# Reading out a state-space scan one step later, and holding a table's transpositions for its rotation table

## The chip, the cores and the metric

One core of one Trainium2 chip runs the whole computation as one program. The metric is the device time of one execution in microseconds (us); three runs of the kernel before gave a median of 2172.66 us (2171.47 to 2174.1).

## The reference

Two layers of a block in which four token mixers work side by side on quarters of the width: latent attention (MLA), grouped-query attention (GQA), a state-space mixer (SSM) and a gated long convolution (hyena). There are 1024 latent and 256 context tokens of width 1024, all in fp32. Cut to what matters here:

```python
for l in range(2):
    h = rms_norm(x) * (1 + scale) + shift          # latent and context
    p = h @ w_in[l]                                # 2912 columns
    a = mla(p); g = gqa(p); s = ssm(p); y = hyena(p)
    x = x + gate * rms_norm(concat(a, g, s, y) @ w_out[l])

# ssm, 16 groups of 16 channels, 64 complex states each, two directions:
bu = einsum('bngh,gph->bngp', u, b_bar)            # drive
s_t = a_bar * s_(t-1) + bu_t                       # linear_scan, over context and then latent tokens
y = einsum('bngp,ghp->bngh', s, c).real            # readout, both directions added
out = gelu(y + d * u) * sigmoid(...) * silu(gate)  # finish
```

## The kernel before

The kernel is written with a tile framework that takes the program's instructions, simulates them with its own clock, and lays down one order for each engine. Each engine then works its list in order and waits at an instruction until the semaphores of what that needs have come. Priorities follow the order in which the code issues things; what is put under `high_priority` goes first, and the scheduler fills the rest of an engine's list with whatever its simulation holds to be ready. So a wait added at one place can shift instructions far from it.

In each layer the stages are: input projection `ipc` (three fp32r matmuls for each fp32 product, from high and low parts of activations and weights), run in blocks of columns of which the last eight, the gates, are written last and are filler for TensorE; hyena's filter (`hps`, `fdft`, `cdft`); the SSM's tables; the SSM's recurrence; hyena's convolution (`hytr`, `ldft`, `lout`; for the context in layer 0 `hcd`, `hco`, `hcz`); the preparation of queries, keys and values (`mqn`, `mkn`, `mv` and others); the SSM's finish (`sglu`); then attention (`aS`, `acx`, `apt`, `apo`), the output projection and the next layer's normalisation. Between the stages data pass through HBM, and all loads and stores (L201) are issued by SP, one list in order. The lanes stand in the order state space, preparation, finish, hyena in layer 0, and hyena, state space, preparation, finish in layer 1. A stage's pools reuse the memory of earlier ones and wait for them.

**Tables** (`ssm_tables`, four groups of four): for each group VectorE and GpSimd form E and Fm (`sE`, `sF`), three products and sums each for the real and the imaginary part. TensorE transposes E (`etp`, L253; eight transpositions for a group), ScalarE copies the result, E times C gives the short kernel (`kfp`). Then the rotation table `tab` (`sT`) is formed in the same way from two tables of powers. E, Fm and their transposed copy have one buffer each. `mtp` builds the direct term's matrices from all groups, and everything goes to HBM.

**Recurrence** (`ssm`, eight steps of two groups): `drive` loads the step's tables, multiplies U by E^T (`drv`) and copies the drive into D in scan order. `scan` turns D by the rotation table (products `cm` on GpSimd, the others on VectorE), runs the two scans (`sV`), and turns the states back into D (`sD`). `read` adds, in one PSUM tile `sy`, the direct term `smt` x U and the states' part `sfm` x D, six matmuls for a step, and ScalarE copies it over U. Step k+1's drive is issued before step k's scan; D has two buffers, Fm (`sfm`) two, the direct term `mt` (`smt`) one. The loop of the kernel before:

```python
d = drive(0)
for gc in range(N):
    e = drive(gc + 1) if gc + 1 < N else None
    yield
    scan(gc, *d)
    yield
    read(gc, d[1], *R)
```

Of the kernel before, what the change touches and what calls it, by code (L numbers as in the profile page):

```python
# [11 lines left out]
F32 = mybir.dt.float32  # L12
# [8 lines left out]
ADD, SUB, MUL = ALU.add, ALU.subtract, ALU.mult  # L21
# [166 lines left out]
class K:  # L188
# [32 lines left out]
        return self.psf.tile([128, 512], F32, tag="f", name=name)  # L221

    def mm(self, out, lhsT, rhs, start=True, stop=True):
        self.keep(self.nc.tensor.matmul(out, lhsT, rhs, start=start, stop=stop))  # L224

    def mm3(self, out, a, b, start, stop):

# [2 lines left out]
        self.mm(out, a[1], b[0], False, stop)  # L230

    def tt(self, out, a, b, op, eng=None):
        self.keep((eng or self.nc.vector).tensor_tensor(out=out, in0=a, in1=b, op=op))  # L233

    def stt(self, out, a, s, b, op0, op1):
        self.keep(self.nc.vector.scalar_tensor_tensor(out=out, in0=a, scalar=s, in1=b, op0=op0, op1=op1))  # L236
# [13 lines left out]

    def tr(self, out, in_):
        p = in_.shape[0]
        self.keep(self.nc.tensor.transpose(out, in_, self.ident[:p, :p]))  # L253


    def setup(self, es):
# [869 lines left out]
    def ssm_tables(self, l, P, poles):  # L1126
# [20 lines left out]
        for gc in range(4):  # L1147
            gs = slice(gc * G, gc * G + G)
            E = P.tile([128, 2, G, 8, 16], F32, tag="sE", name="sE")
            Fm = P.tile([128, 2, G, 8, 16], F32, tag="sF", name="sF")  # L1150
            sh = [128, G, 8, 16]
            for dst, pk, vec, sg in ((E, pe, bb, 1.0), (Fm, pf, cw, -1.0)):
                kr, ki = (pk[:, i, :, gs].rearrange("p t g -> p g t").unsqueeze(3).to_broadcast(sh) for i in range(2))
                vr, vi = (vec[:, i, gs, :].unsqueeze(2).to_broadcast(sh) for i in range(2))
                w1 = P.tile(sh, F32, tag="sw0", name="sw1")
                w2 = P.tile(sh, F32, tag="sw1", name="sw2")
                tt(dst[:, 0], kr, vr, MUL)
                tt(w1, ki, vi, MUL)
                tt(dst[:, 0], dst[:, 0], w1, SUB)
                tt(dst[:, 1], kr, vi, MUL, pool)  # L1160
                tt(w2, ki, vr, MUL, pool)
                if sg > 0:
                    tt(dst[:, 1], dst[:, 1], w2, ADD, pool)
                else:
                    stt(dst[:, 1].rearrange("p g t h -> p (g t h)"), dst[:, 1].rearrange("p g t h -> p (g t h)"), -1.0,
                        w2.rearrange("p g t h -> p (g t h)"), MUL, SUB)

            yield
            et = P.tile([128, 2, G, 128], F32, tag="sET", name="sET")
            for ri in range(2):  # L1170
                ps = self.b1("etp")
                for g in range(G):
                    self.tr(ps[:, g * 128:g * 128 + 128], E[:, ri, g].rearrange("p t h -> p (t h)"))
                nc.scalar.copy(et[:, ri].rearrange("p g c -> p (g c)"), ps)
            self.store(eD[:, :, gs], et)
            self.store(fD[:, :, gs], Fm.rearrange("p r g t h -> p r g (t h)"))
            kp = self.b1("kfp").rearrange("p (g c) -> p g c", c=32)
            for g in range(G):
                for ri in range(2):
                    self.mm(kp[:, g, :], E[:, ri, g].rearrange("p t h -> p (t h)"), cp[:, ri, gc * G + g, :], ri == 0, ri == 1)  # L1180
            nc.vector.tensor_copy(kfb[:, :, gs, :].rearrange("p d g h -> p g d h"),
                                  kp[:, :G, :].rearrange("p g (d h) -> p g d h", d=2))

            tab = P.tile([128, 2, G, 16, 10], F32, tag="sT", name="sT")
            sh = [128, G, 16, 10]
            ar, ai = (big[:, i, gs].unsqueeze(3).to_broadcast(sh) for i in range(2))
            br, bi = (small[:, i, gs].unsqueeze(2).to_broadcast(sh) for i in range(2))
            w1 = P.tile(sh, F32, tag="sw0", name="sr0")
            w2 = P.tile(sh, F32, tag="sw1", name="sr1")
            tt(tab[:, 0], ar, br, MUL)  # L1190
            tt(w1, ai, bi, MUL)
            tt(tab[:, 0], tab[:, 0], w1, SUB)
            tt(tab[:, 1], ar, bi, MUL, pool)
            tt(w2, ai, br, MUL, pool)
            tt(tab[:, 1], tab[:, 1], w2, ADD, pool)
            self.store(tD[:, :, gs], tab.rearrange("p r g a b -> p r g (a b)"))
            yield

        pad = P.tile([128, 352], F32, tag="sw0", name="pad")
# [13 lines left out]
    def ssm(self, l, P, uD, yD, tabs, ctx):  # L1213
# [11 lines left out]
        def readout(gc):  # L1225
            gs = slice(gc * G, gc * G + G)
            Fm = P.tile([128, 2, G, 128], F32, tag="sfm", name="sfm", bufs=2)
            mt = P.tile([128, G, 128], F32, tag="smt", name="smt")
            self.load(Fm, fD[:, :, gs])
            self.load(mt, mD[:, gs])  # L1230
            return Fm, mt
# [11 lines left out]
        def drive(gc):  # L1243
            gs = slice(gc * G, gc * G + G)
            tb = P.tile([128, 2, G, 160], F32, tag="stb", name="stb", bufs=2)
            et = P.tile([128, 2, G, 128], F32, tag="set", name="set")
            self.load(et, eD[:, :, gs])
            self.load(tb, tD[:, :, gs])
            D = P.tile([128, 2, G, 160], F32, tag="sD", name="sD", bufs=2)
            for ri in range(2):  # L1250
                ps = self.b1("drv")[:, :G * 160].rearrange("p (g c) -> p g c", g=G)
                for g in range(G):
                    self.mm(ps[:, g, :], et[:, ri, g, :], U[:, gc * G + g, :])
                nc.scalar.copy(D[0:64, ri], ps[0:64])
                nc.scalar.copy(D[64:128, ri, :, 0:32], ps[64:128, :, 31::-1])
                nc.scalar.copy(D[64:128, ri, :, 32:160], ps[64:128, :, 159:31:-1])
            rt = P.tile([128, G, 160], F32, tag="sR", name="sR", bufs=2)
            for g in range(G):
                self.act(rt[:, g], ones, scale=rho[:, gc * G + g:gc * G + g + 1])
            return tb, D, rt  # L1260

        def scan(gc, tb, D, rt):
# [10 lines left out]
            c0, c1 = temp(0)[..., 0:159], temp(1)[..., 0:159]  # L1273
            tt(c0, V[:, 0], t1, MUL, nc.gpsimd)
            tt(c1, V[:, 1], t1, MUL, nc.gpsimd)
            tt(V[:, 0], V[:, 0], t0, MUL)
            tt(V[:, 1], V[:, 1], t0, MUL)
            f, b = slice(0, 64), slice(64, 128)
            if ctx:
# [6 lines left out]
                if ctx:  # L1286
                    tt(D[b, ri, :, 30::-1], V[b, ri, :, 0:31], c[b, :, 0:31], op)

        def read(gc, V, Fm, mt):
            gs = slice(gc * G, gc * G + G)  # L1290
            n = hi - lo
            ps = self.b1("sy")[:, :G * n].rearrange("p (g c) -> p g c", g=G)
            for g in range(G):
                self.mm(ps[:, g, :], mt[:, g, :], U[:, gc * G + g, lo:hi], True, False)
                self.mm(ps[:, g, :], Fm[:, 0, g, :], V[:, 0, g, lo:hi], False, False)
                self.mm(ps[:, g, :], Fm[:, 1, g, :], V[:, 1, g, lo:hi], False, True)
            nc.scalar.copy(U[:, gs, lo:hi], ps)
# [9 lines left out]

        N = 16 // G
        d = drive(0)
        for gc in range(N):  # L1310
            e = drive(gc + 1) if gc + 1 < N else None
            yield
            scan(gc, *d)
            yield
            read(gc, d[1], *R)
            yield
            if e:
                d, R = e, readout(gc + 1)

    def ssm_finish(self, l, P, uD, yD, ctx):  # L1320
        nc, A = self.nc, self.A
# [689 lines left out]
```

## Time and profile before

| | |
|---|---|
| median of three runs | 2172.66 us |
| the profiled execution's own time | 2168.31 us |
| its span, first to last instruction | 2166.5 us |
| TensorE (PE) busy | 1933.1 us, 89% |
| VectorE (DVE) busy | 1557.0 us, 72% |
| GpSimd (POOL) busy | 972.2 us, 45% |
| ScalarE (ACT) busy | 896.6 us, 41% |

The shares are means over stages with different limits. Layer 0's projections, tables, recurrence and preparation lie in about 75 to 737 us, its attention from 736.8, its output projection from about 1060; in layer 1 the same stretches start at about 1215, 1778 and 2066. The trace holds two records for an fp32 matmul and one for an fp32r matmul, so the counts of `lout`, `hco`, `sglu`, `drv`, `sy` and `etp` in it are twice those of the program; `ipc`, `mkn` and `aS` are counted once.

### The profile page before, as it was taken

To read this page: it belongs to the slowest core of one execution; us is meant where nothing else is said; L and a number is where in the kernel's file an instruction comes from. 1 tells how busy PE (TensorE), PEld (TensorE's weight loads), DVE (VectorE), ACT (ScalarE), POOL (GpSimd) and SP (SyncE) were. 2 spreads that over 40 slices of the span, in tenths; PEclk is the share of its full clock that TensorE was granted. 3 is DMA by queue.
4 is the path that set the end of the run, shared out by engine and by line. 5 is a ranking of instruction groups with operands and counts; after the bars stand their busy time and mean duration, and the time that the engine had idled before them with its cause. 6 is when DMAs were issued, how large, how long until landed. Compare 5 with 4: busy or idle time off the path is not lost.

```text
span 2166.5 us, 31419 instructions
## 1 busy us (share of the span) xinstructions
PE 1933.1 (89%) x10811; PEld 1602.2 (74%) x10811; DVE 1557.0 (72%) x2969; ACT 896.6 (41%) x1926; POOL 972.2 (45%) x782
## 2 busy tenths in 40 slices
PE   6988998899889599899998898988889979999888
PEld 2677887777768477788777677887766667899766
DVE  5699349757776488788653498479769868999721
ACT  2422234224234367667423222344224227788611
POOL 0757236584461144434156558246566624340034
PEclk9798899899999899999899998999899989999999
DMA  7323365337656545452343423364457675561063
GB/s 254 97 91 136 108 222 142 98 118 239 201 174 197 147 126 154 139 160 80 90 142 123 139 99 130 113 232 137 128 161 223 204 213 142 150 169 46 12 184 126
DMA packets 261280, 316.55 MB, mean 146 GB/s; under 512 B 46671, under 2 KB 203599, under 8 KB 257793
## 3 DMA queue, kind: packets, MB, share of 16 engines
q1 hardware_dynamic: 261120, 314.55, 47.6%
q8 instruction: 85, 1.39, 0.3%
q14 instruction: 75, 0.61, 0.1%
HBM read 207.61 MB, written 106.86 MB: 145 GB/s over the span
## 4 chain that ended last, share of the span: by engine, by line
PE 47%; DVE 29%; DMA 10%; issue 7%; POOL 3%; ACT 2%; SPq 2%; POOLq 0%; DVEq 0%; ACTq 0%
PE ipc L224 9%; PE apo L224 7%; PE apt L253 6%; PE aS L224 6%; PE ops L224 6%; DVE lU L233 3%; DVE sD L233 3%; PE mps L224 2%; SPq L201 2%; DVE sp L233 2%; PE acx L224 2%; PE fdft L224 2%; PE hps L224 1%; DVE lX L233 1%; DVE sV L233 1%
## 5 line engine op out<-in xcount | busy, mean ns | idle before, releaser
L224 PE MATMUL ipc<-hh,whi 128*128 128x512 f32 (+2 forms) x992 | 386.7, 390 | 31.4 <-DVE ipt L236 12.8
L224 PE MATMUL ipc<-hh,wlo 128*128 128x512 f32 (+2 forms) x992 | 381.5, 385 | 3.9 <-POOL wlo L233 3.9
L224 PE MATMUL ipc<-hl,whi 128*128 128x512 f32 (+2 forms) x992 | 382.9, 386 | 0.4 <-POOL hl L233 0.4
L224 PEld LDWEIGHTS ipc<-hh,whi 128*128 128x128 f32 x992 | 196.3, 198 | 65.8 <-DVE ipt L236 15.2
L233 DVE TENSOR_TENSOR aPl<-apt,aPh 128x512 fp32r<-128x512 f32 x328 | 223.8, 683 | 20.7 <-ACT aPh L1672 16.9
L1672 ACT CAST aPh<-apt 128x512 fp32r<-128x512 f32 x328 | 186.5, 590 | 124.2 <-PE apt L253 118.3
L224 PEld LDWEIGHTS ipc<-hh,wlo 128*128 128x128 f32 x992 | 196.5, 198 | 35.2 <-POOL wlo L233 4.6
L224 PEld LDWEIGHTS ipc<-hl,whi 128*128 128x128 f32 x992 | 196.9, 198 | 31.2 <-issue 3.8
L233 POOL TENSOR_TENSOR wlo<-wraw,whi 128x512 fp32r<-128x512 f32 x92 | 139.1, 1516 | 137.1 <-ACT whi L462 103.3
L253 PE MATMUL apt<-ident,aP 128*128 128x128 f32 x1312 | 190.5, 276 | 1.2 <-DVE aPl L233 1.0
L224 PE MATMUL aS<-kst,aq 128*128 128x512 f32 x512 | 152.3, 420 | 26.4 <-DMA aq<-gP 20.8
L1637 DVE TENSOR_REDUCE am<-aS 128x1 f32<-128x1024 f32 x128 | 155.5, 1215 | 21.7 <-PE aS L224 21.6
L246 ACT ACTIVATE aP<-aS,am,rs 128x1024 f32<-128x1024 f32 x128 | 155.5, 1215 | 33.5 <-DVE am L243 32.4
L1700 POOL COPY aLB<-am 128x128 f32<-128x128 f32 x72 | 21.0, 292 | 322.8 <-DVE am L1692 322.8
L253 PEld LDWEIGHTS apt<-ident,aP 128*128 128x128 f32 x1312 | 148.3, 141 | 16.7 <-DVE aPl L233 6.4
L224 PE MATMUL apo<-aPh,vst 128*128 128x256 f32 x656 | 138.3, 308 | 15.3 <-ACT aPh L1672 8.7
L224 PE MATMUL apo<-aPl,vst 128*128 128x256 f32 x656 | 123.5, 286 | 1.6 <-DVE aPl L233 1.3
L224 PEld LDWEIGHTS aS<-kst,aq 128*128 128x128 f32 x512 | 88.2, 192 | 41.7 <-issue 21.2
L224 PEld LDWEIGHTS apo<-aPh,vst 128*128 128x128 f32 x656 | 96.2, 190 | 30.6 <-DVE aob L233 15.8
L224 PE MATMUL ops<-owh,omh 128*128 128x512 f32 x288 | 93.5, 405 | 17.1 <-ACT omh L1785 10.8
L224 PEld LDWEIGHTS apo<-aPl,vst 128*128 128x128 f32 x656 | 100.3, 189 | 8.6 <-DVE aPl L233 3.8
L224 PE MATMUL ops<-owl,omh 128*128 128x512 f32 x288 | 93.3, 404 | 0.0
(369 smaller groups left out, 4382.4 us busy)
## 6 DMA issues: line engine op xcount, KB each, us to landing
wraw<-in_w_col_dram SPq DMA_DIRECT2D x64, 256.0 KB
mraw<-in_w_mod_dram SPq DMA_DIRECT2D x32, 512.0 KB
kst<-mK SPq DMA_DIRECT2D x16, 640.0 KB
omx<-mixD SPq DMA_DIRECT2D x18, 512.0 KB
ogt<-gD SPq DMA_DIRECT2D x18, 512.0 KB
k<-kt SPq DMA_DIRECT2D x16, 512.0 KB
lk<-k SPq DMA_DIRECT2D x8, 1024.0 KB
gD<-ipt SPq DMA_DIRECT2D x32, 256.0 KB
```

Of the source, the lines that this page charges most:

```text
L201: return self.nc.sync.dma_start(out=out, in_=in_)
L224: self.keep(self.nc.tensor.matmul(out, lhsT, rhs, start=start, stop=stop))
L233: self.keep((eng or self.nc.vector).tensor_tensor(out=out, in0=a, in1=b, op=op))
L246: self.keep(self.nc.scalar.activation(out=out, in_=in_, func=func, **k))
L253: self.keep(self.nc.tensor.transpose(out, in_, self.ident[:p, :p]))
L1637: self.keep(nc.vector.tensor_reduce(out=x["m"][:, 2 + qi:3 + qi], in_=x["S"][qi], axis=AX.X, op=ALU.max))
L1672: self.keep(nc.scalar.copy(h, ps))
L1700: self.keep(nc.gpsimd.tensor_copy(x["LB"][:, :, o:o + 64], x["m"][:, 10:12].unsqueeze(2).to_broadcast([128, 2, 64])))
```

## The change

The read-out of a step is held back: `scan` becomes a generator that stops after it has issued its product V times t0 (`sV`), and the read-out of the step before is issued there. Its first matmul gets a wait for that product (`behind`, a new dependency between two instructions that share no data). The last read-out follows the loop without a wait. D gets a third buffer and `mt` a second. In the tables the rotation table and its store move ahead of the transpositions, and the group's first transposition waits for the last subtraction of the table's real part. `mm`, `tt` and `tr` return their instruction.

```diff
+    def behind(self, ins, other):
+        self.tc.add_manual_dep(ins.ins, other.ins.name, mybir.DependencyInfo(
+            mybir.DependencyClass.Sync, mybir.DependencyReason.DATA), reason="behind")
...
             yield
+            tab = P.tile([128, 2, G, 16, 10], F32, tag="sT", name="sT")
...
+            last = tt(tab[:, 0], tab[:, 0], w1, SUB)
+            tt(tab[:, 1], ar, bi, MUL, pool)
+            tt(w2, ai, br, MUL, pool)
+            tt(tab[:, 1], tab[:, 1], w2, ADD, pool)
+            self.store(tD[:, :, gs], tab.rearrange("p r g a b -> p r g (a b)"))
             et = P.tile([128, 2, G, 128], F32, tag="sET", name="sET")
             for ri in range(2):
                 ps = self.b1("etp")
                 for g in range(G):
-                    self.tr(ps[:, g * 128:g * 128 + 128], E[:, ri, g].rearrange("p t h -> p (t h)"))
+                    ins = self.tr(ps[:, g * 128:g * 128 + 128], E[:, ri, g].rearrange("p t h -> p (t h)"))
+                    if ri == g == 0:
+                        self.behind(ins, last)
...
-            mt = P.tile([128, G, 128], F32, tag="smt", name="smt")
+            mt = P.tile([128, G, 128], F32, tag="smt", name="smt", bufs=2)
...
-            D = P.tile([128, 2, G, 160], F32, tag="sD", name="sD", bufs=2)
+            D = P.tile([128, 2, G, 160], F32, tag="sD", name="sD", bufs=3)
...
-            tt(V[:, 0], V[:, 0], t0, MUL)
+            yield tt(V[:, 0], V[:, 0], t0, MUL)
...
-        def read(gc, V, Fm, mt):
+        def read(gc, V, Fm, mt, other):
...
-                self.mm(ps[:, g, :], mt[:, g, :], U[:, gc * G + g, lo:hi], True, False)
+                ins = self.mm(ps[:, g, :], mt[:, g, :], U[:, gc * G + g, lo:hi], True, False)
+                if g == 0 and other is not None:
+                    self.behind(ins, other)
...
+        due = None
         for gc in range(N):
             e = drive(gc + 1) if gc + 1 < N else None
             yield
-            scan(gc, *d)
+            half = scan(gc, *d)
+            other = next(half)
+            if due:
+                read(*due, other)
             yield
-            read(gc, d[1], *R)
+            for _ in half:
+                pass
             yield
+            due = gc, d[1], *R
             if e:
                 d, R = e, readout(gc + 1)
+        read(*due, None)
+        yield
```

Three places of the laid-down order follow, first as it was, then as it is. TensorE in layer 0, at the third read-out `sy` of the recurrence; `drv` are drives, `hytr` and `ldft` hyena, `ipc` projections:

```order
L224 MATMUL drv<-sU,set 128x160 x2
L253 MATMUL hytr<-ident,hyx 128x128 x7
L224 MATMUL sy<-sU,smt 128x160
L224 MATMUL sy<-sD,sfm 128x160
L253 MATMUL hytr<-ident,hyx 128x128
L224 MATMUL sy<-sD,sfm 128x160
L224 MATMUL sy<-sU,smt 128x160
L224 MATMUL sy<-sD,sfm 128x160 x2
L224 MATMUL ipc<-bsel,sq 128x2 x7
```

The same place in the changed kernel:

```order
L224 MATMUL ldft<-hyt,hff 128x128 x4
L224 MATMUL sy<-sU,smt 128x160
L224 MATMUL sy<-sD,sfm 128x160 x2
L224 MATMUL sy<-sU,smt 128x160
L224 MATMUL sy<-sD,sfm 128x160 x2
L224 MATMUL drv<-sU,set 128x160 x2
L224 MATMUL ldft<-hyt,hff 128x128 x8
```

The third read-out stood among hyena's transpositions behind the drive of the fourth step; now it stands as one piece behind the drive of the fifth, the first half of the sixth step's drive following it.

SP in layer 0, from the last projections to attention; `hcz` is hyena's context product, `kst`, `vst` and `aq` are attention's keys, values and queries, `gD` a gate's store, `owr` and `mraw` are weights of later stages:

```order
L201 DMA owr<-in_w_out_dram 128x512 x2
L201 DMA gD_78<-ipt 128x256
L201 DMA owr<-in_w_out_dram 128x512 x2
L201 DMA mraw<-in_w_mod_dram 128x1024 x2
L201 DMA mixD_77<-hcz_5082 128x256
L201 DMA mraw<-in_w_mod_dram 128x1024
L201 DMA gpre<-in_g_pre_dram 128x8
L201 DMA bmt<-in_b_modT_dram 128x16
L201 DMA mixD_77<-hcz_5090 128x256
L201 DMA kst<-gP_4000 64x2560 x2
L201 DMA vst<-gV_4001 128x10x192
L201 DMA aq<-gP_4000 64x2x256 x6
```

The same place in the changed kernel:

```order
L201 DMA mixD_77<-sth 128x256 x2
L201 DMA gD_78<-ipt 128x512
L201 DMA mixD_77<-hcz_5082 128x256
L201 DMA mixD_77<-hcz_5090 128x256
L201 DMA gD_78<-ipt 128x512
L201 DMA kst<-gP_4000 64x2560 x2
L201 DMA vst<-gV_4001 128x10x192
L201 DMA gD_78<-ipt 128x256
L201 DMA aq<-gP_4000 64x2x256 x6
L201 DMA owr<-in_w_out_dram 128x512 x4
L201 DMA mraw<-in_w_mod_dram 128x1024 x3
```

Both stores of `hcz` now stand together, and `owr` and `mraw` behind the first queries. On TensorE of layer 0 the last eight `hco`, which feed `hcz`, had nothing between them and attention; now 28 `ipc` stand there.

TensorE in layer 1, where attention begins; `sglu` is the finish of the state-space mixer:

```order
L224 MATMUL ipc<-hh,whi 128x512
L224 MATMUL ipc<-hl,whi 128x512
L224 MATMUL ipc<-hh,wlo 128x512
L224 MATMUL sglu<-sz,sgw 128x256 x4
L224 MATMUL aS<-kst,aq 128x512 x4
L224 MATMUL sglu<-sz,sgw 128x256 x4
L224 MATMUL acx<-kst,aq 128x256 x4
```

The same place in the changed kernel:

```order
L224 MATMUL ipc<-hh,whi 128x512
L224 MATMUL ipc<-hl,whi 128x512
L224 MATMUL ipc<-hh,wlo 128x512
L224 MATMUL sglu<-sz,sgw 128x256 x4
L224 MATMUL aS<-kst,aq 128x512 x4
L224 MATMUL sglu<-sz,sgw 128x256 x12
L224 MATMUL acx<-kst,aq 128x256 x4
```

Of the sixteen `sglu` of this layer, the earlier ones had `ipc` between them; now all sixteen stand behind the last `ipc`. Between the last `mkn` of the preparation and the last `ipc` stood 99 `ipc` and 16 `lout`; now 43 `ipc` stand there.

## Rows read from the trace of the kernel before

**Rows 1.** Page, part 1: busy us (share of the span) xinstructions, by engine

```profile
PE 1933.1 (89%) x10811; PEld 1602.2 (74%) x10811; DVE 1557.0 (72%) x2969; ACT 896.6 (41%) x1926; POOL 972.2 (45%) x782
```

**Rows 2.** Stretches: length; PE, PEld, DVE, ACT, POOL busy (instructions); PEclk, DMA share, GB/s

```profile
250.00:300.00 50.00, 47.55 (x279) 40.23 (x278) 5.56 (x18) 14.05 (x36) 7.20 (x9) 1.00 0.42 129
350.00:400.00 50.00, 38.54 (x199) 34.18 (x197) 49.11 (x56) 13.38 (x36) 34.56 (x31) 0.90 0.42 115
1450.00:1500.00 50.00, 43.09 (x274) 39.26 (x273) 48.81 (x69) 26.34 (x62) 31.93 (x27) 0.96 0.71 234
1550.00:1750.00 200.00, 175.12 (x833) 134.74 (x832) 163.16 (x216) 62.93 (x142) 136.81 (x95) 0.96 0.63 194
1750.00:1790.00 40.00, 29.82 (x123) 23.30 (x121) 20.91 (x53) 11.40 (x27) 0.20 (x1) 0.83 0.84 229
```

**Rows 3.** Who TensorE waited for: us in total, times, longest us

```profile
PE sy L224 <- DVE sD L233: 17.5, 12, 5.4
...
PE sy L224 <- POOL wlo L233: 5.9, 2, 4.2
...
PE etp L253 <- DVE sE L233: 4.4, 2, 3.7
...
PE sy L224 <- POOL dd L233: 2.6, 1, 2.6
...
PE etp L253 <- ACT hsq L246: 2.4, 1, 2.4
```

**Rows 4.** Tile sD, 290 to 430: ns min/median/max, first and last start, forms

```profile
L224 PE MATMUL sy<-sD,sfm x64: 299/299/632, 309.9 to 417.3; 128*128 128x160 f32 x64
L233 DVE TENSOR_TENSOR sD<-sV,cm x48: 215/475/2357, 307.4 to 415.9; 64x318 f32<-64x318 f32 x16, 64x256 f32<-64x256 f32 x16, 64x62 f32<-64x62 f32 x16
...
L233 DVE TENSOR_TENSOR sD<-sD,stb x16: 475/492/1552, 298.1 to 407.1; 128x320 f32<-128x320 f32 x16
```

**Rows 5.** Tile sU, 270 to 300: its loads on SP

```profile
L201 SPq DMA_DIRECT2D sU<-uD x32: 303/429/1337, 274.8 to 291.1; - x32
```

**Rows 6.** Chain of waits, end of layer 0: start us, us, what

```profile
708.24 3.34 PE ipc L224 x26
...
713.10 1.58 PE hco L224 x6
...
715.15 7.03 DMA mixD<-hcz
...
722.75 0.33 SPq L201
...
726.86 9.78 DMA aq<-gP
...
736.77 2.05 PE aS L224 x4
```

**Rows 7.** DMA between 711 and 740 us: sum, and two kinds of load

```profile
DMA packets 4428, 7.30 MB, mean 252 GB/s; under 512 B 624, under 2 KB 3056, under 8 KB 4298
...
kst<-gP SPq DMA_DIRECT2D x2, 640.0 KB
...
vst<-gV SPq DMA_DIRECT2D x1, 960.0 KB
```

**Rows 8.** Chain of waits, whole span: a load by itself

```profile
972.67 2.35 DMA aq<-mS
```

**Rows 9.** Tile mkn, 1600 to 1760: TensorE's instructions

```profile
L224 PE MATMUL mkn<-sp,ukvh x16: 278/283/287, 1636.3 to 1736.7; 128*128 128x256 f32 x16
```

**Rows 10.** Tile sgy, 1740 to 1790: its loads on SP

```profile
L201 SPq DMA_DIRECT2D sgy<-yD x8: 319/395/545, 1746.3 to 1778.9; - x8
```

**Rows 11.** Chain of waits, end of layer 1

```profile
1750.99 3.06 PE lout L224 x24
...
1756.93 5.13 PE ipc L224 x22
...
1784.70 3.80 PE sglu L224 x8
```

More of the change, by code (lines that the diff above doesn't have):

```diff
@@ L223, in mm @@
     def mm(self, out, lhsT, rhs, start=True, stop=True):
-        self.keep(self.nc.tensor.matmul(out, lhsT, rhs, start=start, stop=stop))
+        ins = self.nc.tensor.matmul(out, lhsT, rhs, start=start, stop=stop)
+        self.keep(ins)
+        return ins
     def mm3(self, out, a, b, start, stop):
@@ L232, in tt @@
     def tt(self, out, a, b, op, eng=None):
-        self.keep((eng or self.nc.vector).tensor_tensor(out=out, in0=a, in1=b, op=op))
+        ins = (eng or self.nc.vector).tensor_tensor(out=out, in0=a, in1=b, op=op)
+        self.keep(ins)
+        return ins
+    def behind(self, ins, other):
+        self.tc.add_manual_dep(ins.ins, other.ins.name, mybir.DependencyInfo(
+            mybir.DependencyClass.Sync, mybir.DependencyReason.DATA), reason="behind")
     def stt(self, out, a, s, b, op0, op1):
@@ L252, in tr @@
         p = in_.shape[0]
-        self.keep(self.nc.tensor.transpose(out, in_, self.ident[:p, :p]))
+        ins = self.nc.tensor.transpose(out, in_, self.ident[:p, :p])
+        self.keep(ins)
+        return ins
     def setup(self, es):
@@ L1168, in ssm_tables @@
             yield
+            tab = P.tile([128, 2, G, 16, 10], F32, tag="sT", name="sT")
+            sh = [128, G, 16, 10]
+            ar, ai = (big[:, i, gs].unsqueeze(3).to_broadcast(sh) for i in range(2))
+            br, bi = (small[:, i, gs].unsqueeze(2).to_broadcast(sh) for i in range(2))
+            w1 = P.tile(sh, F32, tag="sw0", name="sr0")
+            w2 = P.tile(sh, F32, tag="sw1", name="sr1")
+            tt(tab[:, 0], ar, br, MUL)
+            tt(w1, ai, bi, MUL)
+            last = tt(tab[:, 0], tab[:, 0], w1, SUB)
[3 more added lines that the diff above has]
+            self.store(tD[:, :, gs], tab.rearrange("p r g a b -> p r g (a b)"))
             et = P.tile([128, 2, G, 128], F32, tag="sET", name="sET")
@@ L1182, in ssm_tables @@
                                   kp[:, :G, :].rearrange("p g (d h) -> p g d h", d=2))
[L1184 to L1196, printed above, removed]
             yield
```

## Prediction

> **What bounds the kernel now.** I read the busy shares first, then the stretches in which the change lies, then who waits for whom, then the chain of waits at the two places where a layer passes from its projections to attention. TensorE is busy for 89% of the span, VectorE for 72% [rows 1], so at first sight whatever takes a wait from TensorE is won. The stretches say otherwise. While the state-space recurrence runs beside the hyena convolution, VectorE has no idle time left: 49.11 of 50 us in layer 0, 48.81 of 50 in layer 1, with TensorE at 38.54 and 43.09 there [rows 2]. So TensorE's waits in this part are paid for VectorE's work, and they end when that work ends, wherever the waiting instruction stands. In 250 to 300 us it is the other way round: VectorE 5.56, TensorE 47.55 [rows 2]. TensorE's waits that the edit aims at are 17.5 + 5.9 + 2.6 = 26.0 us in front of `sy` (read-outs) and 4.4 + 2.4 = 6.8 us in front of `etp` (table transpositions) [rows 3]. 32.8 us is 1.5% of the span, and the most that the edits by themselves can give.
>
> **The change part by part.** The number of instructions is the same on every engine. What moves is their order, and the scheduler's answer to two new waits reaches far beyond the edited lines.
>
> *Read-outs.* In the row of TensorE, read-out k stood behind the drive of step k+1; it now stands behind that of step k+2, all six matmuls together. The states that it reads come from one step earlier, so that wait is gone, and the new one is for VectorE's V times t0 in the middle of the next scan. Behind a waiting `sy` stand the next drive, hyena transforms and projection matmuls, and for the drive wait ScalarE's copies and then GpSimd and VectorE of the scan after it. The matmuls of eight read-outs lie between 309.9 and 417.3 us, 15.3 us a step [rows 4]. But VectorE needs from its first scan instruction at 298.1 to the last at 415.9 [rows 4] whatever TensorE does, and the last two read-outs of each layer have no further step behind which to hide: in layer 0 they now stand next to each other. Ends: 0 (all of the wait comes back at the last read-outs) and -26.0. I take -4, near the zero end, as the row nearest to it is VectorE at 49.11 of 50.
>
> *Buffers and loads of the read-outs.* The third D and the second mt cost memory only. The mt and Fm loads for a read-out now wait in SP's queue for an older read-out; behind them stand the next step's table loads and weight loads. A load lands in 2.35 us when little is ahead of it [rows 8] and a step is 15.3 us: 0, with a step lost (15.3) only if the queue stands still until the read-out wants them.
>
> *Table transpositions.* The first `etp` of layer 0 stands 110 TensorE instructions later, the last one 88; in layer 1 the last stands 43 later. In place of `sE` they wait for the last subtraction of VectorE's rotation table, behind the six products of E and Fm, so by then E is long there. The stall of 6.8 goes, but each group's E buffer is now held until table, transposition and product are through, and the layer's table chain ends later. Ends: -6.8 and, if that chain delays the recurrence by as much, +6.8. I take -2: VectorE, which the recurrence needs, idles between the tables and the recurrence anyhow (5.56 of 50 busy in 250 to 300 [rows 2]).
>
> *What the scheduler puts in the gap.* With the tables later, the hyena loads stand ahead of the 32 loads of U, which took SP from 274.8 to 291.1, 16.3 us [rows 5]; they stood behind them before. VectorE then begins with hyena and takes the scan after it. Its work up to the last scan is the same sum, so I count 0, with ends of -16.3 (VectorE starts that much earlier) and +16.3 (the scan starts that much later, and nothing fills the place).
>
> *End of layer 0.* Here a queue order changes with a clear price. Before, the last inverse transforms `hco` are the very last matmuls in front of attention, and on SP seven large weight loads (four `owr`, three `mraw`) stand around the hyena store and ahead of the keys and queries. TensorE ends `hco` at 713.10 + 1.58 = 714.68 and starts attention at 736.77 [rows 6]: 22.1 us. 8.07 of it go by until SP issues the second store of hyena's product at 722.75, of which 7.03 are the first store, since there is one buffer; 4.1 until the `aq` load that TensorE waits for, behind the keys and values (726.86 - 722.75); 9.78 until that lands [rows 6]. Now 28 gate matmuls stand behind `hco`, and the seven loads stand behind `aq`. From the same point, with a store of 2.35 to 7.03 and an `aq` of 2.35 to 9.78: 8.07 - 7.03 + 2.35 + 4.1 + 2.35 = 9.8 at least, 21.9 at most. Of 26 gate matmuls the chain shows 3.34 us [rows 6], so the 28 moved ones are worth 3.6 more if VectorE has `hcU` ready that much sooner. Ends: 22.1 - 21.9 = -0.2 and 22.1 - 9.8 + 3.6 = -15.9. I take -8: the store is freed of its neighbours, while keys and values (2 x 640 and 960 KB, 2.2 MB [rows 7]) still stand ahead of `aq`. The displaced `mraw` loads are wanted by the first `mps`, which stands 120 TensorE instructions into attention as before; those are their cover.
>
> A rule bears on this term. The trace shows 7.30 MB moved at a mean of 252 GB/s in 711 to 740 us [rows 7]. The Trainium skill, "DMA: Bandwidth & Descriptors", Queues, rings and completion order, says that each DMA engine takes the descriptors of one ring in their order, so a small load pays for the bytes issued ahead of it; the slow store and `aq` against 2.35 agree with that. By this rule `aq` cannot land before keys and values have, 2.2 MB at 252 GB/s or 8.9 us, and the term would be about -4; by the landing of a lone load it would be -12.
>
> *End of layer 1.* This speaks against the change. The last `mkn` of the key preparation stands 72 TensorE instructions later. Ahead of it now are 56 gate matmuls at 5.13/22 = 0.233 us and the 16 last `lout` (3.06/24 x 32 records = 4.1, as the trace has two records for each of them): 13.0 + 4.1 = 17.1 us [rows 11]. Behind it only 43 gate matmuls (10.0 us) are left, and none between the sixteen `sglu` of the state-space output. That lane cannot begin before the preparation's memory is free: its first load was issued at 1746.3 and its last `sglu` ended at 1784.70 + 3.80 = 1788.5 [rows 10, 11], 42.2 us of loads and short vector work that TensorE now has little to cover with. It gets back what VectorE spent on hyena between `mkn` (1736.7 [rows 9]) and that load, 9.6 us, of which I leave 2.6 to the copy, the store and the loads ahead of it that stay: 7; and the 72 instructions fill idle time of TensorE earlier, of which 200 - 175.12 = 24.9 us lie in 1550 to 1750 [rows 2]; I let them fill a quarter, 6. 17.1 - 7 - 6 = +4. Ends: 17.1 - 7 - 12.4 = -2 (half the idle time filled) and +17.1.
>
> *Sum.* -4 - 2 + 0 - 8 + 4 = -10. The profiled execution took 2168.31 us (span 2166.5 and 1.8 around it), 4.35 below the median of the runs, 2172.66. So 2158.3 against the profiled one, and 2162.7 against the median: I predict 2163.
>
> **The rivals.** *All waits go* (chance 0.10): TensorE never waits at either place, VectorE finds the time elsewhere, and layer 0's end gives its -8: -32.8 - 8 + 4 = -37, 2136. For it: VectorE idles 28% of the span. Against it: not in these stretches [rows 2].
>
> *The new wait takes the place of the old* (0.23): the read-outs meet V times t0 as late as they met the states, because the scheduler placed them by its own clock and not by VectorE's; the two layer ends cancel (-4 and +4): 2172. For it: twelve waits for `sD` in the old order [rows 3] show that this clock runs ahead of VectorE.
>
> *The output lane of layer 1 is bared* (0.22, slower): the last `mkn` comes the full 17.1 later, nothing of it fills idle time, and the 42.2 us run beside 10 us of matmuls. With -4 at layer 0's end, -2 at the tables and 0 for the read-outs: 17.1 - 7 - 4 - 2 = +4, and with the late tables at +6.8 instead of -2 it is +13: 2177 to 2186, about 2181. It decides from the point at which the last `mkn` starts more than 12 us later against the layer's start than now. For it: TensorE was busy for only 29.82 of the last 40 us even with the gate matmuls between the `sglu` [rows 2].
>
> **How the numbers follow.** My forecast has 0.45. Its own range, with the terms of the two layer ends half way to their ends together (about 10 to either side), is 2153 to 2173. For 8 in 10 I reach into both neighbours and leave out the far part of the first and the last rival: 2146 to 2182. A measurement of this kernel can tell 0.2% (4.3 us) from no change. Faster than that: 0.45 + 0.10 = 0.55; within it 0.23; slower 0.22.
>
> **What would show it.** Right: waits of TensorE for `sD` at `sy` shrink from 17.5 to a few us and some turn up behind `sV`, most at the last two read-outs; VectorE stays near 49 of 50 in the recurrence; attention of layer 0 starts some 14 us after the last `hco` instead of 22.1, with the hyena store landing in under 5; the stretch in front of layer 1's attention shows more idle TensorE than the 10.2 us of 1750 to 1790. Wrong: the store and `aq` as slow as before; the last `mkn` of layer 1 over 12 us later; or the stretch between tables and recurrence longer by as much as the stalls were.

## The result, and the profile after

The changed kernel is slower: 2188.01 us median (2182.49 to 2202.2) against 2171.47 us (2167.84 to 2174.1), nine runs each, ratio 1.009 (1.0073 to 1.0106; the two medians alone give 1.0076). The forecast was 2163 in 2146 to 2182. The profiled execution is the fastest of the nine, 2182.49 us, so its trace shows a little less than the mean loss.

Shares of the span, part 1 of the page [rows 1]: TensorE is busy 5 us more, VectorE 17.5 us less. So the loss is waiting, and not work.

```profile
PE 1938.2 (89%) x10811; PEld 1613.4 (74%) x10811; DVE 1539.5 (71%) x2969; ACT 901.3 (41%) x1926; POOL 965.5 (44%) x782
```

The same five stretches of the changed kernel as in [rows 2], in the same columns. VectorE is still full in the recurrences (48.26 and 48.92 of 50); in the last row, 1750 to 1790, in front of layer 1's attention, TensorE falls from 29.82 to 19.30 of 40 us, at a granted clock of 0.71 (0.83 before):

```profile
250.00:300.00 50.00, 50.00 (x321) 45.65 (x319) 7.41 (x21) 20.16 (x46) 8.49 (x9) 1.00 0.52 173
350.00:400.00 50.00, 38.86 (x240) 36.02 (x238) 48.26 (x71) 18.18 (x49) 33.65 (x38) 0.91 0.45 120
1450.00:1500.00 50.00, 39.46 (x229) 36.92 (x228) 48.92 (x56) 17.55 (x47) 33.41 (x26) 0.86 0.48 140
1550.00:1750.00 200.00, 175.94 (x856) 138.40 (x856) 150.58 (x209) 59.42 (x135) 123.30 (x86) 0.96 0.58 181
1750.00:1790.00 40.00, 19.30 (x64) 13.78 (x62) 16.81 (x33) 7.91 (x19) 7.03 (x4) 0.71 0.96 265
```

Whom TensorE waited for, as [rows 3]: read-outs 17.1 us (`sV`, `sD`, issue) in place of 26.0, transpositions 3.6 in place of 6.8 and more. At the head stands `ipc` behind VectorE's `rs`, 17.1 us where it was 7.2. Two of its three waits, 7.77 us ending at 338.66 and 8.68 us ending at 403.54, lie in layer 0's recurrence: there the waiting went over from the read-outs to another row. Next is `sglu`, 14.5 us behind `sz` where it was 5.2, and further down `aS` (7.4 us, ending at 1773.7; its releaser is inferred, `aS` reads keys and queries). These two lie in the state-space output of layer 1:

```profile
PE ipc L224 <- DVE rs L532: 17.1, 3, 8.7
PE sglu L224 <- DVE sz L245: 14.5, 3, 8.1
...
PE sy L224 <- DVE sV L235: 11.8, 3, 8.0
...
PE aS L224 <- DMA sgy<-yD: 7.4, 1, 7.4
...
PE etp L262 <- DVE sT L235: 3.6, 2, 2.7
...
PE sy L224 <- DVE sD L235: 3.1, 1, 3.1
...
PE sy L224 <- issue: 2.2, 1, 2.2
```

The chain at the end of layer 0, as [rows 6]: from the end of the last `hco` (703.75 + 3.45 = 707.20) to attention at 723.79 it is 16.6 us, where it was 22.1; 3.8 of them are the 28 gate matmuls. `aq` lands 9.35 us after its issue, hardly sooner than before (9.78):

```profile
703.75 3.45 PE hco L224 x16
707.20 3.79 PE ipc L224 x28
...
714.31 9.35 DMA aq<-gP
...
723.79 2.04 PE aS L224 x4
```

The end of layer 1, as [rows 9 to 11]: tile `mkn`, then the `sgy` loads, then the chain of waits (start us, us, what). Its first line is the place at which the last `mkn` stood before, 72 places ahead of where it stands now.

```profile
L224 PE MATMUL mkn<-sp,ukvh x16: 279/283/415, 1629.3 to 1749.7; 128*128 128x256 f32 x16
```

```profile
L201 SPq DMA_DIRECT2D sgy<-yD x8: 320/398/1945, 1755.7 to 1791.6; - x8
```

```profile
1734.71 1.76 PE mqr L224 x10
...
1759.29 12.62 DMA vst<-gV
...
1780.76 5.96 DMA sgg<-uD
...
1792.04 2.97 DMA sgg<-uD
...
1797.55 3.56 PE sglu L224 x8
...
1808.38 0.50 PE apo L224 x2
```

And the first projection of layer 1, before and after: tile `ipc` from 1100 us, first and last start.

```profile
L224 PE MATMUL ipc<-hh,whi x440: 279/392/828, 1208.8 to 1768.5; 128*128 128x512 f32 x109, 128*128 128x384 f32 x30, 128*128 128x256 f32 x8
```

```profile
L224 PE MATMUL ipc<-hh,whi x440: 275/393/828, 1197.0 to 1759.2; 128*128 128x512 f32 x109, 128*128 128x384 f32 x30, 128*128 128x256 f32 x8
```

Layer 1 begins 11.8 us earlier (1197.0 for 1208.8), and its state-space output ends at 1797.55 + 3.56 = 1801.1 where it ended at 1788.5 [rows 11]. Counted from the layer's first projection that is 24.4 us more, twice what this pair of profiles shows as layer 0's gain.

Read off each run's trace: start of layer 0's attention, and then, as distances from layer 1's first projection, the first hyena transposition `hytr`, the first transposition for the preparation (`prt`), the end of the last `mkn`, of the last `sglu`, and the first `apo` of attention. A row is one execution, and some lie off the median of their runs (e14's is 8.8 us faster, e4's 6.6 us slower); the ratio is from all runs.

| run | layer 0 | hytr | prt | mkn | sglu | apo | ratio to before (95%) |
|---|---|---|---|---|---|---|---|
| before | 736.8 | 257.6 | 372.2 | 528.3 | 579.6 | 586.5 | 1 |
| after | 723.8 | 243.3 | 385.3 | 553.0 | 604.1 | 610.8 | 1.0090 (1.0073 to 1.0106) |
| e1 | 727.5 | 258.0 | 372.7 | 529.7 | 580.2 | 586.9 | 0.9979 (0.9967 to 0.9990) |
| e2 | 735.5 | 257.9 | 372.6 | 551.2 | 602.7 | 609.7 | 1.0107 (1.0094 to 1.0120) |
| e3 | 725.9 | 243.6 | 385.5 | 546.6 | 595.6 | 602.5 | 1.0039 (1.0026 to 1.0052) |
| e4 | 731.2 | 245.1 | 386.1 | 557.3 | 592.8 | 606.9 | 1.0053 (1.0035 to 1.0071) |
| e5 | 736.8 | 256.1 | 376.5 | 535.8 | 596.7 | 603.9 | 1.0078 (1.0061 to 1.0096) |
| e6 | 724.1 | 243.4 | 383.7 | 544.3 | 599.5 | 606.4 | 1.0047 (1.0030 to 1.0064) |
| e7 | 733.2 | 257.9 | 372.5 | 529.1 | 579.7 | 586.7 | 0.9980 (0.9968 to 0.9992) |
| e8 | 733.8 | 257.8 | 372.5 | 538.2 | 596.8 | 603.6 | 1.0064 (1.0043 to 1.0084) |
| e9 | 728.7 | 240.9 | 382.2 | 536.6 | 587.6 | 594.4 | 1.0033 (1.0017 to 1.0048) |
| e10 | 731.1 | 241.3 | 382.6 | 540.1 | 582.1 | 599.1 | 1.0060 (1.0044 to 1.0077) |
| e11 | 729.8 | 257.8 | 372.1 | 529.3 | 573.9 | 589.0 | 0.9997 (0.9985 to 1.0009) |
| e12 | 727.4 | 241.0 | 382.2 | 540.9 | 587.7 | 599.0 | 1.0048 (1.0030 to 1.0066) |
| e13 | 737.1 | 260.1 | 368.0 | 522.6 | 580.6 | 590.6 | 0.9998 (0.9983 to 1.0013) |
| e14 | 722.8 | 260.5 | 368.2 | 516.8 | 567.9 | 582.2 | 0.9963 (0.9948 to 0.9978) |

From `apo` to the program's last matmul it is 360.8 to 364.9 us in all of them: what is lost is lost before that point.

### The profile page after: what moved, and what is told of

Its sections match the earlier page's. It is cut to its first block, busy times and chain, and to the rows that moved or that the text cites. A ratio compares the mean times of both kernels' runs of the same rounds, so it can differ in the third digit from the quotient of the medians.

```text
span 2180.7 us, 31461 instructions
## 1 busy us (share of the span) xinstructions
PE 1938.2 (89%) x10811; PEld 1613.4 (74%) x10811; DVE 1539.5 (71%) x2969; ACT 901.3 (41%) x1926; POOL 965.5 (44%) x782
## 4 chain that ended last, share of the span: by engine, by line
PE 49%; DVE 22%; DMA 9%; issue 7%; POOL 6%; SPq 3%; ACT 3%; POOLq 0%; DVEq 0%; ACTq 0%
PE ipc L224 11%; PE apo L224 7%; PE ops L224 6%; PE aS L224 6%; PE apt L262 6%; SPq L201 3%; DVE sD L235 2%; DVE lU L235 2%; PE mps L224 2%; PE acx L224 2%; PE fdft L224 1%; DVE sp L235 1%; PE hps L224 1%; PE lout L224 1%; DMA modg<-msb 1%
## 5 line engine op out<-in xcount | busy, mean ns | idle before, releaser
L224 PE MATMUL ipc<-hh,whi 128*128 128x512 f32 (+2 forms) x992 | 387.6, 391 | 40.5 <-DVE rs L532 17.1
L224 PE MATMUL ipc<-hl,whi 128*128 128x512 f32 (+2 forms) x992 | 382.2, 385 | 0.4 <-POOL hl L235 0.4
L235 POOL TENSOR_TENSOR wlo<-wraw,whi 128x512 fp32r<-128x512 f32 x92 | 133.9, 1460 | 161.0 <-ACT whi L473 159.5
L224 PE MATMUL apo<-aPh,vst 128*128 128x256 f32 x656 | 138.4, 309 | 15.3 <-ACT aPh L1695 8.8
L224 PEld LDWEIGHTS apo<-aPh,vst 128*128 128x128 f32 x656 | 96.3, 190 | 30.4 <-DVE aob L235 15.8
L346 POOL CAST mhi<-mraw 128x1024 fp32r<-128x1024 f32 x32 | 33.3, 1041 | 136.8 <-PE mps L224 53.9
```

What stands on the lines that cost most here:

```text
L224: ins = self.nc.tensor.matmul(out, lhsT, rhs, start=start, stop=stop)
L235: ins = (eng or self.nc.vector).tensor_tensor(out=out, in0=a, in1=b, op=op)
L346: nc.gpsimd.tensor_copy(hi, raw)
```

## The experiments

Theory A: the loss is made in layer 1, where the scheduler's new order ends the preparation later and the attention waits for what follows; layer 0 gains at its own end. Rival B: read-outs and tables cost it themselves, through their waits, in both layers. The edits use one helper, an order without a wait: `ins` stands behind `other` in the list of an engine that both use.

```diff
+    def place(self, ins, other):
+        self.tc.add_manual_dep(ins.ins, other.ins.name, mybir.DependencyInfo(
+            mybir.DependencyClass.NoSync, mybir.DependencyReason.DATA), reason="place")
```

The edits below leave out the lines that fill the lists: `seq` has all matmuls so far, the gates last, and `mkn`, `glu`, `ht` (`hytr`), `dr` (`drv`) and `at[...]` (loads) have the instructions of one tile in the order of issue. The scheduler lays down the rest of the order anew in each run, so other instructions can move too.

**e1, which layer.**

`early` moves the rotation table, `late` the read-outs; the buffers follow `late`, the second mt as the third D.

```diff
+            early = l == 0
...
+            D = P.tile([128, 2, G, 160], F32, tag="sD", name="sD", bufs=3 if l == 0 else 2)
...
+        late = l == 0
```

> Both edits in layer 0 alone; layer 0's order of every engine is that of the changed kernel, layer 1's that of the kernel before. Theory A (the loss is made at the end of layer 1, layer 0 gains at its own end): the 13.0 us by which attention of layer 0 starts earlier (736.8 to 723.8) stay to the end, ratio to before 0.994, about 2158 us. Rival B (read-outs and tables themselves cost in the recurrence, half of the 16.5 us in each layer): ratio 1.004, about 2180.

Ratio 0.9979: a gain of 0.21%, 4.6 us, a third of what the one pair of profiles shows (736.8 to 723.8). So layer 1 loses 1.009 - 0.9979 = 1.1%, 24 us. A holds in its sign and place, not in layer 0's size.

**e2, the late end alone, in the kernel before.**

```diff
+        if l == 1:
+            k.place(k.mkn[-6], k.seq[-44])
```

> The kernel before, with neither edit; in layer 1 the last six mkn are ordered behind the gate matmul that has 43 behind it, so 56 gate matmuls go ahead of the preparation's end and none are left between the sglu, as in the changed kernel. Theory A: the preparation ends some 13 to 17 us later and the state-space output runs bare, 13 to 20 us slower, ratio 1.006 to 1.009. Rival B: filler has only moved, 0 to 3 us.

23.6 us (2192.52 against 2168.93), ratio 1.0107: the whole loss of layer 1 without either edit, and more than A said. Its last `mkn`, and whom TensorE waited for from 1740 us:

```profile
L225 PE MATMUL mkn<-sp,ukvh x16: 274/283/283, 1639.0 to 1760.4; 128*128 128x256 f32 x16
```

```profile
PE sglu L225 <- DVE sz L244: 17.9, 3, 11.5
PE aS L225 <- DMA aq<-gP: 6.5, 1, 6.5
```

The preparation begins where it did (372.6 for 372.2); the last `mkn` is 22.9 us later (551.2 for 528.3), attention 23.2. So a late end of the preparation reaches attention whole, and it takes none of B's waits to lose that much.

**e3, the end restored in the changed kernel.**

```diff
+            s = k.glu[-16:]
+            for i, other in ((120, k.mkn[-1]), (60, s[1]), (46, s[3]), (19, s[7])):
+                k.place(k.seq[-i], other)
```

> The changed kernel; in layer 1 the last 120 gate matmuls are ordered behind the last mkn, and 60, 46 and 19 of them behind the second, fourth and eighth sglu, so the last mkn stands at about its place of before. Theory A: 13 to 20 us come back, 2168 to 2175. Rival B: unchanged, 2188.

11 us come back (1.0039), about half of layer 1's loss. The last `mkn` stands at about its old place, but ends only 6.4 us earlier than in the changed kernel: TensorE now waits ahead of it, 2.01 and 4.37 us in front of two `lout` for VectorE's `lX` (hyena), 1.01 us in front of `mv`. So something ahead of it is late as well. The two don't add up: late by the gates alone the last `mkn` is 22.9 us behind (e2), without them 18.3 us (e3), with both 24.7 us (after).

**e4, the bulk loads behind the small ones.**

```diff
+            for x in [k.at[l, "ald"][0]] + k.at["owr"][-16:][:4] + k.at["mraw"][-8:][:3]:
+                k.place(x, k.at[l, "sgg"])
```

`at[l, "ald"][0]` is the first load of keys, `at[l, "sgg"]` the last `sgg`.

> The changed kernel; in layer 1 the first keys, the first owr and mraw loads are ordered behind the last sgg load on SP; TensorE's order is the same but for 8 places. If the second and later rounds of the state-space output are held up by the keys and values ahead of their loads (16.0 us from the first to the second round of sglu, against 8.3 in the kernel before), the lane gets 5 to 8 us shorter and the time falls to 2180 to 2184, unless attention then waits for its keys. If the lane is set by the late preparation alone: 2188, or slower by the 9 us that keys and queries take to land.

1.0053, 8 us less than the changed kernel. First to last `sglu` is 22.7 us (1773.9 to 1796.6), where it was 38.3:

```profile
L225 PE MATMUL sglu<-sz,sgw x32: 379/634/795, 1773.9 to 1795.9; 128*128 128x256 f32 x32
```

So the second round's loads did stand behind keys and values: in the changed kernel's chain above, 12.62 us of `vst` lie ahead of them. But attention then waits for its keys and queries: from the last `sglu` to `apo` it is 14.1 us, 6.7 in the changed kernel.

**e5 and e6, one edit each** (switches as in e1, both layers).

> Read-outs held back in both layers, with the third D and second mt; the tables as before. Layer 1's last mkn stands 22 TensorE instructions later than before (77 gate matmuls behind it, 20 between the sglu). Theory A (the end of layer 1 decides, 23.6 us for 72 places; layer 0 gives 5): 7 - 5 = +2 us, ratio 1.001. Rival B (the edit decides by the waits it takes away or adds): the wait for the states of 17.5 us becomes smaller, and the time falls by up to that, ratio 0.992; or the new waits cost it back, 1.000 in both layers alike.

1.0078; A's count of 2 us was wrong. The edit does what it says: waits at `sy` are 8.9 us in place of 27.1 (26.0 in [rows 3], and 1.1 in two smaller rows),

```profile
PE sy L224 <- DVE sV L235: 6.7, 4, 3.3
...
PE sy L224 <- ACT sD L1277: 1.6, 1, 1.6
...
PE sy L224 <- issue: 0.6, 2, 0.4
```

and no time comes of it. In layer 0 attention starts at 736.8, as before; in layer 1 `mkn` is 7.5 us late and the output lane takes 42.0 us from its first to its last `sglu`, 33.9 before. 18 us of waits are taken away, and the kernel is 17 us slower.

The lane's 8 us can be read off SP's list (start us, us). Four `owr` and two `mraw` now stand ahead of the last round's loads; in the kernel before that round's loads, from 1777.74, stand ahead of `owr` (1780.44) and `mraw` (1784.10). TensorE then waits 13.6 us for the last round's `sz`. No run took these loads away from e5; e4 is the nearest to it.

```profile
1785.26 1.01 SPq L201 DMA_DIRECT2D owr<-in_w_out_dram  x2
...
1788.38 0.92 SPq L201 DMA_DIRECT2D mraw<-in_w_mod_dram  x2
1790.01 0.33 SPq L201 DMA_DIRECT2D sgy<-yD  x1
```

```profile
PE sglu L224 <- DVE sz L245: 13.6, 1, 13.6
```

> The rotation table ahead of the transpositions in both layers, with the new wait; read-outs and buffers as before. Layer 1's last mkn stands 49 TensorE instructions later than before, 66 gate matmuls behind it and none between the sglu. Theory A: 16 - 5 = +11 us, ratio 1.005. Rival B: 6.8 us of waits at the transpositions gone or doubled, ratio 0.997 to 1.003.

1.0047, as A had it. Hyena's first transposition moves from 257.6 to 243.4 us, `prt` from 372.2 to 383.7: it is this edit that moves hyena's begin.

**e7, the loads at the end of layer 0, in the kernel before.**

```diff
+        if l == 0:
+            for x in k.at["owr"][:4] + k.at["mraw"][:3]:
+                k.place(x, k.at[l, "ald"][8])
```

`at[l, "ald"]` has two `kst`, `vst`, then the `aq`; number 8 is the sixth `aq`.

> The kernel before; at the end of layer 0 alone the first four owr and three mraw loads are ordered behind the sixth aq load on SP, as the changed kernel has it; TensorE's order in layer 0 is unchanged. If the seven loads slowed the hyena store and the queries: the store takes 2.4 us in place of 7.03, aq still some 9 us behind keys and values, attention of layer 0 starts 17 us after the last hco in place of 22.1, 5 us faster, ratio 0.998. If they don't matter: store and start as before, ratio 1.000.

0.998, as expected if the seven loads mattered. SP's issues (start us, us), and TensorE's wait, 15.4 us in place of 20.8:

```profile
716.96 2.59 SPq L202 DMA_DIRECT2D mixD<-hcz  x2
719.65 1.15 SPq L202 DMA_DIRECT2D kst<-gP  x2
...
721.71 6.01 SPq L202 DMA_DIRECT2D aq<-gP  x6
728.64 4.20 SPq L202 DMA_DIRECT2D mraw<-in_w_mod_dram  x3
733.05 2.11 SPq L202 DMA_DIRECT2D owr<-in_w_out_dram  x4
```

```profile
PE aS L225 <- DMA aq<-gP: 15.4, 1, 15.4
```

**e8, half the dose of e2** (`k.seq[-72]`).

> The kernel before; as e2, but only 28 gate matmuls more go ahead of the last six mkn in layer 1 (71 left behind). Theory A as a straight line through e2: 28/72 of 23.6 = 9 us, ratio 1.004. If the place counts only by its 28 x 0.233 = 6.5 us of matmuls, 6.5, ratio 1.003; if what counts is that no cover is left, and 71 matmuls are cover enough: 0.

1.0064, 14 us: `mkn` is 9.9 us late, attention 17.1, more than a straight line. Of the 7.2 us between them, 3.1 are lost up to the first `sglu`, whose input is there at 1760.2 while TensorE works gate matmuls until 1764.05. 4.1 are lost in the lane, whose last loads stand behind `owr` and `mraw` as in e5. Of the 71 matmuls left, 54 stand ahead of the first `sglu` and 17 between the `sglu`; the kernel before had 51 and 48.

**e9, e10, e12, what is left after e3; e11, e4's order on e1.**

```diff
+        if l == 1:
+            k.place(k.inv[-1], k.pre)
```

In e9 this stands beside e3's order; `inv[-1]` is the last add of hyena's inverse transforms on VectorE, `pre` the preparation's last instruction there (layer 1).

> The changed kernel; in layer 1 hyena's last inverse transform on VectorE is ordered behind the preparation's last VectorE instruction, and the gate matmuls as in e3 (120 behind the last mkn, 60, 46 and 19 behind three of the sglu). If the rest of the loss that e3 left (8.5 us) is hyena's last block, which VectorE now works ahead of the preparation's end: the last mkn comes 10 to 15 us earlier than in e3 and the time falls to that of layer 0 changed alone, ratio to before 0.998. If the preparation is already late when it begins (its first mkn 396.6 us after the layer's start, 381.7 before): no earlier than e3 by more than 3 us, ratio 1.003.

1.0033 is the second answer in time. In the order the first one came as well: the last `mkn` ends at 536.6, 10.0 us earlier than in e3. But it is still 8.3 us later than before, and the preparation begins 10.0 us late (382.2 for 372.2): what is left is there when it begins.

e10 is the edits of e3 and e4 together:

> The changed kernel with the orders of e3 and e4 together. If the late preparation and the bulk loads ahead of the second round's loads are two costs, both come back, 11 + 8 us: ratio 1.000. If each only uncovers the other (attention waits for its keys once the lane is short): as e3, ratio 1.004.

1.006, no better than e3 (the intervals overlap). Each of the two costs uncovers the other: the lane takes 26.8 us, but from its end to `apo` it is 17.0.

e12 is e9's order without e3's:

> The changed kernel; in layer 1 hyena's last inverse transform on VectorE is ordered behind the preparation's last VectorE instruction, nothing is ordered on the gates (51 stand behind the last mkn, 3 between the sglu). If VectorE's order makes the late preparation: as e9. If the gate matmuls ahead of it do: as the changed kernel, ratio 1.009. If both: between, 1.004.

1.0048, between the two: both the gates and VectorE's order make the end late.

e11, both edits in layer 0 only as e1, and e4's order in layer 1:

> Both edits in layer 0 alone as in e1; in layer 1, whose order is that of the kernel before, the keys, owr and mraw loads are ordered behind the last sgg load as in e4. If the bulk loads hold up the lane of the kernel before too (33.9 us from its first to its last sglu; 22.7 in e4): 11 us less lane, 5 more for the keys, ratio 0.9979 - 0.003 = 0.995. If the 48 gate matmuls between its sglu set its length, or the keys' landing takes back all: ratio 0.998.

0.9997, slower than either answer and no gain on e1 (0.9979). The lane ends earlier than in e1 (573.9 for 580.2), but attention gets its keys and queries later (`apo` 589.0 for 586.9).

**e13 and e14, hyena's begin in layer 1.** In the kernel before, hyena's first transposition stood in the middle of the recurrence's fifth drive (36 records of `drv` ahead of it, 8 to a drive), in the changed one behind the third (24). With the tables later, one of the filter's six blocks on VectorE is left between the recurrence's scans, where there were two, and hyena starts earlier.

```diff
+        if l == 1:
+            k.place(k.ht[32], k.dr[32 + 19])
```

`ht[32]` is the layer's first `hytr`, `dr[32 + 19]` the last matmul of its fifth drive, half a drive later than in the kernel before.

> The changed kernel; in layer 1 hyena's first transposition is ordered behind the fifth drive of the recurrence, as in the kernel before (it stood behind the third, ahead of all read-outs). The scheduler then leaves 68 gate matmuls behind the last mkn and none between the sglu. If hyena's earlier begin delays the preparation: its first transposition 372 to 375 us after the layer's start in place of 382 to 385, ratio 1.004. If not (the tables or read-outs themselves do it): 382 or more, ratio 1.006 to 1.009.

0.9998 (0.9983 to 1.0013): one order edge gives the whole net loss back, more than was expected. `prt` is at 368.0 and `mkn` at 522.6, earlier than before the change; 4.1 us of layer 1's loss are left at `apo` (590.6 for 586.5). The edge doesn't move hyena alone: the scheduler then leaves 68 gate matmuls behind the last `mkn`, where the changed kernel has 43. At 0.233 us each [rows 11] these 25 are an estimated 5.8 us of the 30.4 by which `mkn` comes earlier. The 17.3 us at `prt` are not theirs: in all three kernels the same 428 `ipc` of the layer are still to come there. First starts of `hytr`, then of `prt`, in layer 1, of before, after and e13:

```profile
L253 PE MATMUL hytr<-ident,hyx x32: 270/272/300, 1466.4 to 1632.8; 128*128 128x128 f32 x32
```

```profile
L262 PE MATMUL hytr<-ident,hyx x32: 270/273/476, 1440.4 to 1608.8; 128*128 128x128 f32 x32
```

```profile
L271 PE MATMUL hytr<-ident,hyx x32: 270/272/273, 1470.6 to 1643.0; 128*128 128x128 f32 x32
```

```profile
L253 PE MATMUL prt<-ident,rs x10: 272/273/274, 1581.1 to 1719.1; 128*8 128x128 f32 x10
```

```profile
L262 PE MATMUL prt<-ident,rs x10: 270/272/273, 1582.3 to 1736.5; 128*8 128x128 f32 x10
```

```profile
L271 PE MATMUL prt<-ident,rs x10: 271/272/273, 1578.5 to 1717.1; 128*8 128x128 f32 x10
```

What hyena's begin does shows in the stretch from 190 us after the layer's first projection to about the preparation's first transposition, of before, after and e13, columns as [rows 2]:

```profile
1398.80:1580.00 181.20, 158.19 (x901) 141.84 (x900) 136.36 (x207) 60.67 (x142) 101.75 (x72) 0.92 0.49 154
```

```profile
1387.00:1580.00 193.00, 160.07 (x881) 144.34 (x880) 146.24 (x208) 60.63 (x142) 110.95 (x81) 0.88 0.47 145
```

```profile
1400.50:1580.00 179.50, 155.28 (x888) 138.67 (x887) 127.83 (x194) 61.55 (x145) 96.42 (x71) 0.92 0.52 158
```

VectorE does 9.9 us more in it after the change (146.24 for 136.36), and 8.5 less than before in e13. The work on tile `lU` of hyena's transforms, which the preparation doesn't need, is 26.48 us before, 44.27 after and 24.36 in e13 (the same stretches, busy us of VectorE and then GpSimd on this tile):

```profile
1398.80:1580.00 181.20, 26.48 (x29) 15.46 (x11) 0.92 0.49 154
```

```profile
1387.00:1580.00 193.00, 44.27 (x42) 25.89 (x18) 0.88 0.47 145
```

```profile
1400.50:1580.00 179.50, 24.36 (x27) 14.49 (x10) 0.92 0.52 158
```

TensorE has about the same busy time (160.07 for 158.19) in 11.8 us more, at a granted clock of 0.88 for 0.92.

e14 has the orders of e13, e9 and e3 together:

> The changed kernel with the orders of e13 and e9. If these two are the whole loss of layer 1: layer 1 as long as before, layer 0's gain left, ratio 0.998. If the read-outs' or tables' own waits cost something in layer 1: ratio 1.001 to 1.003.

0.9963 (0.9948 to 0.9978), medians 2163.07 against 2169.85 us (0.9969): faster than both kernels. With both edits in both layers, layer 1 is 4.3 us shorter to `apo` than before the change (582.2 for 586.5, in the fastest of its runs). So the loss doesn't lie in the edits' own waits, as B has it; whether these cost a little that the orders outweigh is not shown. The last `mkn` starts at 1712.0, 37.7 us earlier than in the changed kernel:

```profile
L226 PE MATMUL mkn<-sp,ukvh x16: 278/282/552, 1617.1 to 1712.0; 128*128 128x256 f32 x16
```

With the order of layer 1 in hand, the changed kernel gains 0.3 to 0.4%, 7 to 8 us. Whether the edits or the orders earn it in layer 1 is open: e1, which leaves layer 1 as it was, has 0.9979 with an overlapping interval, and the orders were not tried in the kernel before.

## Why the prediction was wrong

*The step that failed is "End of layer 1",* +4 with ends -2 and +17.1. It cost 24.4 us in the profile and 24 by the ratios of after and e1. By its own terms:

| term | predicted | measured | from |
|---|---|---|---|
| the row reaches the old place of the last `mkn` (here the `mqr` at 1734.71) | -6 | +9.5 | (1734.71 - 1197.0) - (1737.0 - 1208.8) |
| 72 instructions ahead of it | +17.1 | +15.3 | 1750.0 - 1734.71 |
| from `mkn` to the first `sgy` load | -7 | -3.6 | 5.7 in place of 9.3 |
| the lane from that load to the last `sglu` | 0 | +3.2 | 45.4 in place of 42.2 |

The 72 places cost about what was said, in part by luck: the order had changed further up too, and other instructions stand in them (44 gate matmuls and 10 `mqr` among them). What failed is the belief that the moved instructions would fill idle time of TensorE. Of the 24.9 us idle in 1550 to 1750, 24.1 are still idle after the change. It was waiting for VectorE, 23.0 of it in the kernel before, with `mqn` behind `pv` at the head (6.3); the text had said as much of the recurrence and forgot it 100 us on. And the shift in "What the scheduler puts in the gap" was seen in layer 0 alone and counted 0. It is there in layer 1 too, and there it makes the preparation begin 13.1 us late (385.3 for 372.2), which e13 undoes. The preparation's end is the start of the state-space output, so a late end went through to attention (e2).

*The rival that came true* is the bared output lane (0.22), by its own condition: the last `mkn` over 12 us later against the layer's start; it was 24.7. Its price, 2177 to 2186, left out the 9.5. Its name was half wrong: in e13 no gate matmul stands between the `sglu` either, and they take 33.2 us from first to last (33.9 before). What was paid for is mostly lateness: of the 24.4 us the lane itself has 3.2.

*Read-outs*, -4 of 0 to -26: the waits were worth 0, for the reason given [rows 2, 4]. e5 takes 18 us of them away, and layer 0's recurrence is 116.2 us long on VectorE (297.0 to 413.2) where it was 117.8. What the sum had at nothing is the new order that this edit sets off in layer 1: e5 is 17 us slower. *Tables*, -2: the stall fell to 3.6 as said; the move of hyena that this edit sets off was the dear part (e6). *Buffers*, 0: no run tried them alone.

*End of layer 0*, -8: direction and mechanism right, size smaller: e7 gives 4 us for the seven loads, e1 4.6 for all of layer 0. `aq` still took 9.35 us, so the lower price, about -4, was the right one. That is the price by the rule cited there: the Trainium skill, "DMA: Bandwidth & Descriptors", Queues, rings and completion order, has each DMA engine take one ring's descriptors in order; this trace agrees here (9.35 us with the seven loads gone but keys and values still ahead, 9.78 with all of them), and again at the end of layer 1 (e4). That `aq` "cannot land before" keys and values was too strong: the same section of the Trainium skill says that a later descriptor may finish its write before an earlier one. When the keys landed no trace here shows.

*Range and chances*: 2188 lies 6 us above the range, on the side of a rival that had 0.22 and ended at 2186, because this one slower case was built from layer 1's tail alone.

*What stays open*: why e5, whose hyena starts nearly as before (256.1 for 257.6), loses 7.5 us at the preparation was not taken apart, and its 8 us in the lane are read and not tested. In e13's stretch VectorE's hyena work and the lower clock both go back; how the 11.8 us divide between them is not known. How much of e13's gain behind `prt` is the 25 gate matmuls was not tried apart either.

## What to carry to other kernels

Where one engine waits for another that is busy 49 of 50 us, as here, taking the wait away won no time. Ask instead what a change does to the stage whose end frees the next one, and measure that end from the stage's own start. Where a scheduler lays the order, price the lanes that it moves in every place where the moved step recurs, not only where the first diff shows it. Order edges without waits are a cheap way to find the culprit and to keep it in place, if one checks what else the scheduler moves: three kinds of them turned +0.9% into -0.4%.

## What was not expected of the hardware

The same order of layer 0 reached its attention at 722.8 to 737.1 us in ten profiles (after, e1, e3, e4, e9 to e14; e14 and e13 are the two ends), and the order before at 733.8 to 736.8 in three (before, e2, e8). So one pair of profiles, 736.8 and 723.8, overstated a gain of 4.6 us. Moving bulk loads behind small ones is no free gain: it took 16 us off the lane in e4, and 7.4 of them came back at once as a wait for keys and queries.
